# Splitting twelve weight units of the first mixing stage during the first down-projection

## The chip, the cores and the metric

The program runs on one core of one Trainium2 chip. The metric is the device time of one execution in microseconds (us). The engines named below are TensorE (PE in the profile, with PEld for its weight loads), VectorE (DVE), ScalarE (ACT), GpSimd (POOL) and the sync engine (SP), which issues most of the DMAs. Every engine works through its own list of instructions in the order in which the list was written; an instruction that waits holds up all that stand behind it on the same engine.

## The reference

One encoder layer runs over two independent sequences (`x_prompt` and `x_sample`) of 512 tokens and 1024 channels, with the same float32 weights for both:

```
x = x + 0.5 * swiglu(rms_norm(x, ffn1_norm), w_gate, w_up, w_down)      # D_FF = 2816
h = rms_norm(x, mix_norm)
proj = h @ w_in                        # 1024 x 4880: q, k, v, memory q, k, v, gates, output gate, two merge gates
att = grouped-query attention(proj);  mem = bidirectional mLSTM(proj)
x = x + (sigmoid(g_att) * (att @ w_up_att) + sigmoid(g_mlstm) * (mem @ w_up_mlstm)) @ w_out
x = x + 0.5 * swiglu(rms_norm(x, ffn2_norm), ...)
y = rms_norm(x, final_norm)
```

## The kernel before

Precision: each float32 operand is held as two reduced-precision parts, a high part (the value rounded) and a low part (the rest), and a product is made of three matmuls: high by high, high by low, low by high. Splitting a weight tile therefore costs one ACT instruction (the copy that rounds) and one DVE instruction (the subtraction).

Stages, in order: the up-projections of the first feed-forward block for both sequences; its down-projection `ffn_down`; the mixing stage of `x_prompt` (`mix(0, ...)`), then that of `x_sample` (`mix(1, ...)`); the second feed-forward block in the same two parts.

`ffn_down` works in 28 steps: seven products of a fast (Strassen-like) scheme for each of four chunks of the hidden width, taken in the order of `DOWN` (L539 to L544). A chunk holds three units of hidden rows, the third chunk two. In a step, `products` (L610) goes over four column blocks d, each in one PSUM bank, with three matmuls for each unit. When a block of a step is done, `flush_` (L655) adds the bank into a sum in SBUF: on ACT (L663) for some products of the first chunk, on DVE (L665) otherwise. Several products in a row build on the same bank, so PE may begin block d of the next step only when the flush of block d of this step has read the bank. `prep(i + 2)` (L601) makes the weight units of the step after next: `split` (L713) with ACT (L715) and DVE (L716) into a ring of eight unit buffers, and `load_right(i + 4)` issues the loads of the other operand, which were parked in DRAM, on SP. A unit buffer is free again when PE has ended the step that used it.

`e5` (L553) is a tile of the pool whose slots all have the size of the largest tile, 128 x 8 x 512; it is only half as large as its slot.

In the mixing stage the weights come in units of 128 columns of `w_in`. `load_w` (L281) serves both sequences. For `x_prompt` it loads the raw unit (512 KB, L271 on SP), splits it with ACT (L278) and DVE (L279) into a tile with the tag `w8`, of which there are four, and parks high and low part in DRAM with two DMAs on SP (L303). For `x_sample` the unit is found in the table `parked`, and two DMAs on SP (L293) bring both parts back. The lookup is:

```
if key in parked:
    d, shape = parked[key]
    w2 = wpool.tile(shape, F32R, tag="w8", bufs=4, name=nm("w"))
    for i in range(2):
        nc.sync.dma_start(f(w2[:, i]), d[:, i])
    return w2[:, 0], w2[:, 1]
```

In the attention part of `mix(0, ...)` the units of gates and of memory queries and keys are fed between the steps of the attention, by `among` (L1171) through `proj` (L814), whose matmuls have the lines L825 and L839.

Which order the instructions have on each engine is not the order of the code: a scheduler lays them out, and takes at each moment the instruction with the lowest place in the program (moved by `shifted`) among those that are ready by its own estimate. `pin` keeps some in the order of the program. `mix_consts` (L741) loads tables for the mixing stage on POOL's queue; it is called after step 7 of `ffn_down`.

Of the kernel before, what the change touches and what calls it, by code (L numbers as in the profile page):

```python
# [8 lines left out]
F32 = mybir.dt.float32  # L9
F32R = mybir.dt.float32r  # L10
I32 = mybir.dt.int32
AF = mybir.ActivationFunctionType
ALU = mybir.AluOpType
# [3 lines left out]
P = 128  # L17
S = 512
D = 1024
KD = D // P  # L20
# [6 lines left out]
def encoder(ctx, tc, I, outs):  # L27
    nc = tc.nc
    cpool = ctx.enter_context(tc.tile_pool(name="cpool", bufs=1))
    dpool = ctx.enter_context(tc.tile_pool(name="dpool", bufs=1, space=bass.MemoryType.DRAM))  # L30
# [11 lines left out]
    def nm(s):  # L42
        n_id[0] += 1
        return f"{s}_{n_id[0]}"
# [89 lines left out]
    def A(shape, dtype=F32, name="a"):  # L134
        return apool.tile(shape, dtype, tag="a", name=nm(name))
# [148 lines left out]
    parked = {}  # L284
# [23 lines left out]
    V_ = nc.vector  # L308
# [236 lines left out]
    DH = KD // 2  # L545
    n_steps = len(DOWN) * len(CHUNKS)

    def ffn_down(wd, rb, ring, tail, xres, done, at_step, hook, turned=None):
        n = n_steps
        rt = [A([P, 4, 2, S], F32R, "rt") for _ in range(3)]  # L550
        e16 = xs[2] = A([P, KD, S], F32, "e16")
        xs[0], xs[1] = A([P, KD, S], F32, "xs"), A([P, KD, S], F32, "xs")
        e5 = A([P, DH, S], F32, "e5")  # L553
        right = [[t[:, q] for q in range(3)] for t in rt] + [[t[:, 3] for t in rt]]
        w8 = [wpool.tile([P, 2, 2, S], F32R, tag="w8", bufs=4, name=nm("w")) for _ in range(4)]
        units = [t[:, i] for t in w8 for i in range(2)]
# [2 lines left out]
        free = [(0, t[:, 0:S], t[:, S:D]) for t in wr] + [(1, va, ha), (1, *v2)]  # L559
        s1s = ring.rows["s"]  # L560
        at = [0, 0]

        def load_right(i):
            if i < n:
                for q, fp in enumerate(CHUNKS[i // 7]):
                    nc.sync.dma_start(f(right[(i + 3) % 4][q]), rb[fp][DOWN[i % 7]])
# [13 lines left out]
        def refill():  # L580
            while order and free:
                key = order.pop(0)
                free.sort(key=lambda t: t[0])
                raws_[key] = load_raw(*key)
# [14 lines left out]
        def prep(i):  # L599

            if i >= n:  # L601
                return
            m, c = DOWN[i % 7], CHUNKS[i // 7]
            out = left[i] = []
            if m == T2_ and i > 2:
                sums(c)
            for fp in c:
                src = s1[fp] if m == T1 else raws_[fp, int(m in (B21, T4, B22))][1 + int(m in (T3, T4))]
                u = units[at[0] % 8]
                at[0] += 1  # L610
                split(src, u[:, 0, :], u[:, 1, :])
                out.append(u)
            if m in (T3, B22):
                for fp in c:
                    free.append(raws_.pop((fp, 0 if m == T3 else 1)))
                refill()
# [3 lines left out]
        def products(i, ts, ds=range(DH)):  # L620
            m = DOWN[i % 7]
            first = m in (B11, T2_, T1)
            grp = "Y" if m in (T2_, T3, T4) else "X"
            for d in ds:
                if first:
                    banks[grp, d] = (((PS, PS, PT, PT) if grp == "Y" else (MM, MM, MM, PO))[d])()
                p = banks[grp, d][:, ts]
                us = left[i]
                for q, u in enumerate(us):
                    r = right[(i + 3) % 4][q]  # L630
                    for k, (a, b) in enumerate(((0, 0), (0, 1), (1, 0))):
                        nc.tensor.matmul(p, u[:, a, d * P:(d + 1) * P], r[:, b, ts],  # L632
                                         start=(first and q == 0 and k == 0), stop=(q == len(us) - 1 and k == 2),
                                         skip_group_check=True)
                flush_(i, d, p, ts)

        def products_turned(i):

            us = left[i]
            for b in range(4):  # L640
                cuts = (0, S) if b < 3 else (0, S // 2, S)
                for j, c in enumerate(zip(cuts, cuts[1:])):
                    cs = slice(*c)
                    p = (MM, MM, MM, PO)[b - j]()
                    for q, u in enumerate(us):
                        r = right[(i + 3) % 4][q]
                        for k, (a, h) in enumerate(((0, 0), (0, 1), (1, 0))):
                            nc.tensor.matmul(p[:, cs], r[:, h, b * P:(b + 1) * P], u[:, a, cs],
                                             start=(q == 0 and k == 0),
                                             stop=(q == len(us) - 1 and k == 2), skip_group_check=True)  # L650
                    turned(b, j, len(cuts) - 2 - j, p[:, cs], cs)
# [44 lines left out]
        for i in range(n):  # L696
            if i == n - 1 and turned:
                products_turned(i)
            else:
                products(i, whole)  # L700
            prep(i + 2)
            load_right(i + 4)
            if i == 1:
                free.extend((1, *h4[k:k + 2]) for k in (0, 2))
                refill()
            if i == at_step:
                hook()

    def normed(xt, g, R, d):

        V_.scalar_tensor_tensor(xt, xt, g[:, d:d + 1], R, op0=ALU.mult, op1=ALU.mult)
# [8 lines left out]
    HM, DM = 4, 128  # L720
# [44 lines left out]
    win_v = w_in.rearrange("(k p) c -> p k c", p=P)  # L765
# [674 lines left out]
    def busy(n, idle):  # L1440

        for _ in range(n):
            pin(nc.tensor.matmul(idle, hot[:, 0:P], hot, start=True, stop=True))

    xbuf = [dpool.tile([P, KD, S], F32, name=f"xbuf{s}") for s in range(2)]
    x2buf = [dpool.tile([P, KD, S], F32, name=f"x2buf{s}") for s in range(2)]
    rbuf = [[[dpool.tile([P, 2, S], F32, name=f"rbuf{n}_{j}_{m}") for m in range(7)] for j in range(NF // 2)]
            for n in range(2)]
# [7 lines left out]
    up = Up(xc, I["ffn1_w_gate"][0], I["ffn1_w_up"][0], rbuf[0], 12)  # L1456
# [263 lines left out]
    tail = up.rest(raw0, 13, mix_gains)  # L1720
# [24 lines left out]
    def prep1(d):  # L1745
# [4 lines left out]
        normed(xt, gm, R[1], d)  # L1750
        split(xt, nhl[1][0][:, d, :], nhl[1][1][:, d, :])

    ffn_down(I["ffn1_w_down"][0], rbuf[0], up.ring, tail, xbuf, done1, 7, mix_consts)


    box()
# [56 lines left out]
    up = Up(xc, I["ffn2_w_gate"][0], I["ffn2_w_up"][0], rbuf[1], 10)  # L1813
# [21 lines left out]
    tail = up.rest(raw0)  # L1835
# [68 lines left out]
    def done2(s, d, th):  # L1904
# [5 lines left out]
        elif d == KD - 1:  # L1910
            turn1()

    ffn_down(I["ffn2_w_down"][0], rbuf[1], up.ring, tail, x2buf, done2, n_steps - 7, load_fn, turned=finish1)


# [40 lines left out]
```

## Time and profile before

| what | value |
|---|---|
| time, median of 3 runs | 2035.04 us (2034.21 to 2035.5) |
| the profiled execution | 2037.6 us, span 2035.8 us |
| PE busy | 2020.2 us of the span (99%) |
| DVE busy | 1584.0 us (78%) |
| ACT busy | 921.5 us (45%) |
| POOL busy | 111.1 us (5%) |
| first matmul of `ffn_down` | 437.76 us after the start |
| granted TensorE clock, mean | 0.999 |

The busy time of PE is made of modelled ends: matmuls overlap, so a duration of 389 ns does not mean that one starts every 389 ns. How fast PE goes is read from the starts. A row of a timeline names the start and the length in us, the engine, the line, the operation, what it writes and reads, and the number of equal instructions that it merges; in brackets stand the idle time before it and what ended it. A row of a stretch has, after the two ends and the length, the busy time of each engine with the number of its instructions, then the granted clock, the busy share of the 16 DMA engines, and GB/s.

### The profile page before, as it was taken

How to read it: one execution, taken by the hardware profiler on the slowest of the kernel's cores; microseconds unless marked ns; L12 is line 12 of the kernel's file. 1: busy time of each engine (PE TensorE's matmuls, PEld its weight loads, DVE VectorE, ACT ScalarE, POOL GpSimd, SP SyncE). 2: the span in 40 equal slices, each digit the busy share in tenths (PEclk: the TensorE clock that was granted, in tenths of full speed). 3: DMA queues.
4: the chain of work that ended last, by engine and by line, in shares of the span. 5: the costliest groups of instructions: out<-in, count | busy, mean ns of one | idle time of the engine just before them, and what ended most of it. 6: DMA issues, size and time to landing. Idle time of an engine off the chain costs nothing.

```text
span 2035.8 us, 26777 instructions
## 1 busy us (share of the span) xinstructions
PE 2020.2 (99%) x9185; PEld 1665.7 (82%) x9185; DVE 1584.0 (78%) x2828; ACT 921.5 (45%) x1675; POOL 111.1 (5%) x148
## 2 busy tenths in 40 slices
PE   9999999999999999999999999999999999999998
PEld 7888888888888888888888877888888888888887
DVE  7988888886797798776566867467798988786797
ACT  7644444442234577653325654245444444442224
POOL 0000000001003000100120000011000000000001
PEclk9999999999999999999999999999999999999999
DMA  9656565799766954868656668877565655689753
GB/s 312 197 171 216 177 218 182 237 334 364 271 214 225 294 169 148 259 208 302 211 166 209 214 189 268 274 228 228 173 206 166 217 177 179 205 332 352 269 196 119
DMA packets 334696, 462.17 MB, mean 227 GB/s; under 512 B 21384, under 2 KB 207840, under 8 KB 333280
## 3 DMA queue, kind: packets, MB, share of 16 engines
q1 hardware_dynamic: 329920, 446.08, 65.8%
q0 software_dynamic: 4480, 14.11, 2.0%
q8 instruction: 72, 1.18, 0.2%
q14 instruction: 64, 0.52, 0.1%
q10 hardware_dynamic: 160, 0.27, 0.0%
HBM read 292.44 MB, written 167.94 MB: 226 GB/s over the span
## 4 chain that ended last, share of the span: by engine, by line
PE 91%; DVE 3%; DMA 3%; ACT 2%; issue 1%; SPq 0%; DVEq 0%; ACTq 0%
PE mm L839 13%; PE pso L374 12%; PE pst L374 12%; PE mm L374 10%; PE mm L632 9%; PE pss L374 6%; PE pst L632 4%; PE pss L632 4%; PE mm L825 4%; PE mm L804 3%; PE pso L632 3%; PE pso L1148 1%; PE pss L1101 1%; PE pst L839 1%; PE pss L839 1%; PE pso L1360 1%
## 5 line engine op out<-in xcount | busy, mean ns | idle before, releaser
L374 PE MATMUL pst<-xc,w 128*128 128x512 f32 x1056 | 253.8, 389 | 1.2 <-ACT t L409 1.2
L374 PEld LDWEIGHTS pst<-xc,w 128*128 128x128 f32 x1056 | 198.1, 188 | 42.7 <-ACT t L409 1.6
L374 PE MATMUL mm<-xc,w 128*128 128x512 f32 x972 | 229.6, 390 | 1.6 <-ACT f L382 1.6
L374 PEld LDWEIGHTS mm<-xc,w 128*128 128x128 f32 x972 | 182.0, 188 | 39.6 <-ACT f L382 2.1
L632 PE MATMUL mm<-rt,w 128*128 128x512 f32 x765 | 178.7, 389 | 0.0
L839 PE MATMUL mm<-xh,w 128*128 128x512 f32 x560 | 176.1, 391 | 1.4 <-DMA w<-wpark 1.4
L332 ACT ACTIVATE w<-t 128x512 fp32r<-128x512 f32 x176 | 106.5, 627 | 135.7 <-issue 63.1
L632 PEld LDWEIGHTS mm<-rt,w 128*128 128x128 f32 x765 | 143.5, 188 | 29.8
L333 DVE TENSOR_TENSOR w<-t,w 128x512 fp32r<-128x512 f32 x176 | 117.8, 688 | 40.9 <-ACT w L332 39.1
L374 PE MATMUL pso<-xc,f 128*128 128x512 f32 x528 | 127.0, 389 | 0.0
L374 PE MATMUL pss<-xc,w 128*128 128x512 f32 x528 | 126.8, 389 | 0.0
L374 PE MATMUL pso<-xc,w 128*128 128x512 f32 x528 | 126.8, 389 | 0.0
L839 PEld LDWEIGHTS mm<-xh,w 128*128 128x128 f32 x560 | 104.8, 188 | 23.7 <-DMA w<-wpark 1.8
L374 PEld LDWEIGHTS pso<-xc,f 128*128 128x128 f32 x528 | 99.0, 188 | 21.0 <-DVE t L413 0.4
L374 PEld LDWEIGHTS pso<-xc,w 128*128 128x128 f32 x528 | 99.1, 188 | 20.6
L374 PEld LDWEIGHTS pss<-xc,w 128*128 128x128 f32 x528 | 99.1, 188 | 20.6
L825 PE MATMUL mm<-xh,w 128*128 128x512 f32 x336 | 111.9, 398 | 0.0
L839 PE MATMUL mm<-xl,w 128*128 128x512 f32 x280 | 109.6, 391 | 0.0
L715 ACT ACTIVATE w<-wr 128x512 fp32r<-128x512 f32 x72 | 45.1, 632 | 138.4 <-PE pso L632 64.8
L278 ACT ACTIVATE w<-wr 128x1024 fp32r<-128x1024 f32 (+1 forms) x64 | 65.3, 1030 | 80.4 <-issue 24.5
L279 DVE TENSOR_TENSOR w<-wr,w 128x1024 fp32r<-128x1024 f32 (+1 forms) x64 | 79.8, 1247 | 26.6 <-ACT w L278 15.7
L715 ACT ACTIVATE w<-t 128x512 fp32r<-128x512 f32 x82 | 51.8, 632 | 107.4 <-PE pst L632 62.4
(457 smaller groups left out, 4080.4 us busy)
## 6 DMA issues: line engine op xcount, KB each, us to landing
rt<-rbuf SPq DMA_DIRECT2D x154, 512.0 KB, 5.4
wpark<-w SPq DMA_DIRECT2D x88, 512.0 KB, 3.6
w<-wpark SPq DMA_DIRECT2D x88, 512.0 KB, 5.3
wr<-in_ffn_w_gate_dram SPq DMA_DIRECT2D x62, 512.0 KB, 5.4
rbuf<-tab SPq DMA_DIRECT2D x102, 256.0 KB, 4.0
wr<-in_ffn_w_up_dram SPq DMA_DIRECT2D x44, 512.0 KB, 4.6
rbuf<-f SPq DMA_DIRECT2D x72, 256.0 KB, 4.2
wr<-in_w_in_dram SPq DMA_DIRECT2D x36, 512.0 KB, 5.7
```

The source lines that it names most:

```text
L278: pin(nc.scalar.activation(hi, raw, AF.Copy))
L279: pin(lo_eng.tensor_tensor(lo, raw, f(hi), op=ALU.subtract))
L332: pin(nc.scalar.activation(t[:, 0], src, AF.Copy))
L333: pin(V_.tensor_tensor(t[:, 1], src, f(t[:, 0]), op=ALU.subtract))
L374: nc.tensor.matmul(p, a[:, k, :], xt[:, b, k, :], start=(first and k == 0 and i == 0), stop=(k == HK_ - 1 and i == 2), skip_group_check=True)
L632: nc.tensor.matmul(p, u[:, a, d * P:(d + 1) * P], r[:, b, ts], start=(first and q == 0 and k == 0), stop=(q == len(us) - 1 and k == 2), sk ...
L715: nc.scalar.activation(hi, src, AF.Copy)
L804: mark(nc.tensor.matmul(p[b][:, :N], a[:, k, bs], w_[:, kl, :], start=(k == 0 and i == 0), stop=(k == KD - 1 and i == 2)), (kl, b, i) == ( ...
L825: pin(nc.tensor.matmul(p[0], a[:, k, :], b, start=(k == 0 and i == 0), stop=(k == n - 1 and i == 2)))
L839: mark(nc.tensor.matmul(p, a[:, k, :], b, start=(k == 0 and i == 0), stop=last), last)
L1101: pin(nc.tensor.matmul(p, qT[:, h, b * P:(b + 1) * P], kv[:, hk * 2 + j, :], start=(j == 0), stop=(j == 1)))
L1148: pin(nc.tensor.matmul(pos[h], Vst[:, kb, h // 4, :], w, start=(kb == KBS[0] and i == 0), stop=(kb == KBS[3] and i == 1)))
```

## The change

`ffn_down` gets a list `aside` of twelve units of `w_in`. `e5` is allocated with twice the size, in the same slot, and its upper half is used as two buffers of 512 KB, `lo` and `hi`. After each step from step 10 on, one unit is written into the program: its raw values are loaded into `lo` on POOL's queue, ACT copies them to `hi`, DVE subtracts in place, and two DMAs on POOL's queue park both parts in DRAM under the key that the mixing stage looks up. There is one pair of buffers, so the load of the next unit overwrites what the two DMAs of this one read. In `mix(0, ...)` these twelve units are then found in `parked`: the raw load, the split and the two parking DMAs are gone there, and two loads stand in their place. `mix(1, ...)` is unchanged. Only the call in the first block passes a list.

```
-    def ffn_down(wd, rb, ring, tail, xres, done, at_step, hook, turned=None):
+    def ffn_down(wd, rb, ring, tail, xres, done, at_step, hook, turned=None, aside=()):
...
-        e5 = A([P, DH, S], F32, "e5")
+        e5_ = A([P, KD, S], F32, "e5")
+        e5, spare = e5_[:, 0:DH], e5_[:, DH:KD].rearrange("p (i a) c -> p i (a c)", i=2)
...
+        aside = list(aside)
+
+        def split_aside(view, key):
+            lo, hi = [spare[:, i].rearrange("p (k c) -> p k c", c=view.shape[2]) for i in range(2)]
+            nc.gpsimd.dma_start(lo, view)
+            nc.scalar.activation(hi.bitcast(F32R), lo, AF.Copy)
+            V_.tensor_tensor(lo.bitcast(F32R), lo, hi, op=ALU.subtract)
+            shape = [P, 2] + list(view.shape[1:])
+            parked[key] = d, _ = dpool.tile(shape, F32, name=nm("wpark")), shape
+            for i, t in enumerate((hi, lo)):
+                nc.gpsimd.dma_start(d[:, i], t)
...
             if i == at_step:
                 hook()
+            if i >= ASIDE and aside:
+                split_aside(*aside.pop(0))
+
+    ASIDE = 10
...
-    ffn_down(I["ffn1_w_down"][0], rbuf[0], up.ring, tail, xbuf, done1, 7, mix_consts)
+    ffn_down(I["ffn1_w_down"][0], rbuf[0], up.ring, tail, xbuf, done1, 7, mix_consts,
+             aside=[(win_v[:, :, c:c + P], ("in", c)) for c in
+                    (896, 1408, *(2832 + d * P for d in range(2)), *(2320 + h * P for h in range(HM)),
+                     *(2832 + d * P for d in range(2, 6)))])
```

In the changed kernel the lines behind the change have other numbers: the flushes are L676 (ACT) and L678 (DVE), the unit splits L732 (ACT) and L733 (DVE), the parts of the new function L568 (load), L569 (ACT), L570 (DVE) and L574 (parking).

Where the scheduler put this is seen at three places. POOL's list around the tables of the mixing stage, before (`hn` is the last of the small loads of the stage ahead, L744 to L754 are `mix_consts`):

```order
L738 TENSOR_SCALAR hn<-hn 128x4
L744 DMA tab_4218<-in_c_tri_dram 128x512
L745 DMA tab_4218<-in_c_mask_dram 128x256
L747 DMA f_302_4221<-in_c_rope_dram 128x8x64
L750 DMA gb_4223<-in_q_norm_dram 128x64
L752 TENSOR_SCALAR gb_4223<-gb_4223 128x64
```

and now (`e` is the tile of the two buffers):

```order
L755 TENSOR_SCALAR hn<-hn 128x4
L568 DMA e_276_3694<-in_w_in_dram 128x8x128
L574 DMA wpark_4393<-e_276_3694 128x1024 x2
L568 DMA e_276_3694<-in_w_in_dram 128x8x128
L574 DMA wpark_4453<-e_276_3694 128x1024 x2
L568 DMA e_276_3694<-in_w_in_dram 128x8x128
L761 DMA tab_4218<-in_c_tri_dram 128x512
L762 DMA tab_4218<-in_c_mask_dram 128x256
L764 DMA f_302_4221<-in_c_rope_dram 128x8x64
L767 DMA gb_4223<-in_q_norm_dram 128x64
L574 DMA wpark_4509<-e_276_3694 128x1024 x2
```

Two units and the load of a third stand ahead of the tables, though the program writes the tables three steps earlier; load and parking follow each other in turns, and the other nine units follow behind.

ACT's list at the end of step 0 of `ffn_down` (the flush of its last block, from the bank `pso`), before:

```order
L663 ACTIVATE e_273_3691<-pso_3811 128x512
L715 ACTIVATE w_3695<-wr_3701 128x512
L715 ACTIVATE w_3696<-wr_3701 128x512
L715 ACTIVATE w_3697<-wr_3702 128x512
L715 ACTIVATE w_3697<-t_18_279 128x512
```

and now:

```order
L676 ACTIVATE e_273_3691<-pso_3811 128x512
L569 ACTIVATE e_276_3694<-e_276_3694 128x1024
L732 ACTIVATE w_3695<-wr_3701 128x512
L732 ACTIVATE w_3696<-wr_3701 128x512
L732 ACTIVATE w_3697<-wr_3702 128x512
L732 ACTIVATE w_3697<-t_18_279 128x512
```

The first of the twelve copies stands behind the flushes of step 0, not behind step 10, and the unit splits of step 3 and 4 behind it; the other eleven follow at distances of three to six unit splits at first, and four at the end.

DVE's list around the twelfth of the subtractions (`mm` and `pso` of 45xx are the banks of step 15, `pss_4660` and `pss_4668` those of the first two blocks of step 16):

```order
L678 SCALAR_TENSOR_TENSOR xs_3692<-mm_4572,xs_3692 128x512
L678 SCALAR_TENSOR_TENSOR xs_3692<-mm_4580,xs_3692 128x512
L570 TENSOR_TENSOR e_276_3694<-e_276_3694 128x1024
L678 SCALAR_TENSOR_TENSOR xs_3692<-pso_4588,xs_3692 128x512
L733 TENSOR_TENSOR w_3697<-t_6_267,w_3697 128x512
L678 SCALAR_TENSOR_TENSOR e_273_3691<-pss_4660,e_273_3691 128x512
L733 TENSOR_TENSOR w_3697<-t_7_268,w_3697 128x512
L678 SCALAR_TENSOR_TENSOR e_273_3691<-pss_4668,e_273_3691 128x512
```

The subtraction is new there; the flushes of step 15 and 16 and the unit splits stand around it in the order that they had before.

## The prediction

> **What bounds the kernel now.** I read the totals of the page first, then the busy time by stretch, then the starts of the matmuls.
>
> ```profile
> span 2035.8 us, 26777 instructions
> PE 2020.2 (99%) x9185; PEld 1665.7 (82%) x9185; DVE 1584.0 (78%) x2828; ACT 921.5 (45%) x1675; POOL 111.1 (5%) x148
> ```
>
> PE is busy in 99% of the span: a wait that PE does not have today is paid in full, and work that leaves ACT, DVE or SP gains only what PE idles for it. The profiled execution is 2037.6 us, its span and 1.8 us outside it, and lies 2.6 us above the median of 2035.04; I add the sum to the span and carry it over to the median. About 0.2% (4 us) is what a measurement of this kernel can tell from no change.
>
> By stretch (after the ends and the length: busy time and number of instructions, granted clock, DMA share, GB/s): three of `ffn_down`, and the attention of `mix(0, ...)`.
>
> ```profile
> core 0: us, PE busy (x) PEld busy (x) DVE busy (x) ACT busy (x) POOL busy (x), PEclk, DMA share, GB/s
> 437.80:494.90 57.10, 57.10 (x254) 47.28 (x253) 41.92 (x65) 22.38 (x39) 8.67 (x12) 1.00 0.98 367
> 494.90:552.00 57.10, 57.10 (x253) 47.28 (x252) 38.60 (x60) 13.29 (x21) 0.00 (x0) 1.00 0.75 267
> 552.00:590.00 38.00, 38.00 (x169) 31.48 (x168) 32.61 (x53) 8.81 (x14) 0.00 (x0) 1.00 0.69 242
> 690.00:800.00 110.00, 109.75 (x543) 89.47 (x542) 100.19 (x202) 73.57 (x142) 0.00 (x0) 1.00 0.58 192
> ```
>
> The place that work is taken from, 690 to 800, has a PE that idles 0.25 us; the place that it goes to has a PE that never idles, and in its first 57 us DMA engines that are full already (0.98).
>
> Two starts of steps, by PE's timeline:
>
> ```profile
> 437.76 6.28 PE L632 MATMUL mm<-rt,w 128*128 128x512 f32 x27
> 445.92 6.28 PE L632 MATMUL mm<-rt,w 128*128 128x512 f32 x27
> 552.00 4.24 PE L632 MATMUL mm<-rt,w 128*128 128x512 f32 x18
> 557.44 4.24 PE L632 MATMUL mm<-rt,w 128*128 128x512 f32 x18
> 568.32 2.88 PE L632 MATMUL pss<-rt,w 128*128 128x512 f32 x12
> ```
>
> A step of three units takes 8.16 us, one of two units (steps 14 to 20) 5.44 us. Step 14 begins at 552.00, step 17 at 568.32.
>
> **What the change takes from the mixing stage.** Twelve copies, twelve subtractions, twelve raw loads and 24 parkings, by the row for the raw tile and the one for the parked parts between 690 and 800:
>
> ```profile
> L279 DVE TENSOR_TENSOR w<-wr,w x13: 1201/1218/1227, 690.0 to 791.7; 128x1024 fp32r<-128x1024 f32 x13
> L278 ACT ACTIVATE w<-wr x12: 1040/1058/1062, 689.7 to 790.6; 128x1024 fp32r<-128x1024 f32 x12
> L271 SPq DMA_DIRECT2D wr<-in_w_in_dram x12: 384/452/1826, 693.5 to 783.5; - x12
> DMA to landing us min/median/max: 4.4/4.7/8.1
> ```
>
> ```profile
> L303 SPq DMA_DIRECT2D wpark<-w x26: 319/320/704, 689.9 to 793.0; - x26
> DMA to landing us min/median/max: 2.6/3.2/4.7
> ```
>
> That is 12 x 1.06 = 12.7 us of ACT and 12 x 1.22 = 14.6 us of DVE, all under a PE that idles 0.25 us in 110 us. The matmuls of these units stand in the groups by shape with 1.4 us lost over the whole program:
>
> ```profile
> L839 PE MATMUL mm<-xh,w 128*128 128x512 f32 x560 | 176.1, 391 | 1.4 <-DMA w<-wpark 1.4
> ```
>
> Since ends are modelled, some idleness may hide in the busy time: PE misses 15.6 us (2035.8 - 2020.2) in the whole span, of which a share by length (110 / 2035.8) is 0.8 us. I put the gain at 1.5 us, between none and 3 us (twice the 1.4 of the row).
>
> **What it adds: a chain through one buffer pair.** By the order, ACT's first copy stands behind the flush of step 0, the twelfth subtraction on DVE between the flushes of step 15. ACT and DVE take their instructions in order, so each copy that is not ready holds up the flushes and unit splits behind it, and PE waits for those. The rows at both ends, of ACT and of DVE, and that of the unit splits around them:
>
> ```profile
> 447.35 0.61 ACT L663 ACTIVATE e<-pso 128x512 f32<-128x512 f32 x1
> ```
>
> ```profile
> 562.18 1.31 ACT L715 ACTIVATE w<-t 128x512 fp32r<-128x512 f32 x2 [4.08 <-PE pso L632]
> ```
>
> ```profile
> 563.45 0.69 DVE L665 SCALAR_TENSOR_TENSOR xs<-pso,xs 128x512 f32<-128x512 f32 x1
> ```
>
> The first copy can begin at 447.35 + 0.61 = 448.0; its load, issued when the buffer is free at about 437.8, has ten microseconds. The latest start of the twelfth without harm: behind its subtraction DVE has the flush of step 15's last block, a unit split and the flush of step 16's first block, which PE needs at 568.3. Three at 0.69 are 2.1, the subtraction 1.22, the copy 1.06, two handovers about 0.2: 568.3 - 4.6 = 563.7, and I take 563. So eleven cycles must fit into 563 - 448 = 115 us, 10.45 us for each. (The same reckoning gives 506 for the sixth, so the line is nearly straight.)
>
> A cycle is: raw load, copy, subtraction, handover to POOL, landing of the low part's parking, since the next load overwrites what that reads. The floor of it, with the fastest landings of the rows above and the one place where POOL sends what DVE has just made:
>
> ```profile
> 1047.74 0.69 DVE L1426 SCALAR_TENSOR_TENSOR f<-mm,f 128x512 f32<-128x512 f32 x1
> ```
>
> ```profile
> 1048.73 0.56 POOL L1427 DMA_DIRECT2D x2buf<-f  x1 [4.86 <-DVE f L1426]
> ```
>
> DVE ends at 1048.43, so the handover is 0.30. Floor: 4.4 + 1.06 + 1.22 + 0.30 + 2.6 = 9.6 us. That is only 0.85 us under the allowance, and it has no load from others and SP's issue times in it. POOL's own, from the tables of the mixing stage:
>
> ```profile
> 467.88 0.60 POOL L744 DMA_DIRECT2D tab<-in_c_tri_dram  x1 [134.76 <-DMA wr<-in_ffn_w_down_dram]
> 469.02 0.91 POOL L747 DMA_DIRECT2D f<-in_c_rope_dram  x1
> ```
>
> The second moves 128 x 8 pieces, like a raw unit: 0.91 against SP's 0.45 above, +0.5, so 10.1. Then the load of the DMA engines. The operand `rt` (512 KB, as here) landed thus from 500 to 600 and from 445 to 500:
>
> ```profile
> L566 SPq DMA_DIRECT2D rt<-rbuf x38: 319/320/627, 501.9 to 598.4; - x38
> DMA to landing us min/median/max: 3.2/4.4/6.0
> ```
>
> ```profile
> L566 SPq DMA_DIRECT2D rt<-rbuf x21: 319/320/447, 445.3 to 495.1; - x21
> DMA to landing us min/median/max: 5.8/8.6/13.8
> ```
>
> After 500 the median is 1.2 above the minimum; on both legs that is 10.1 + 2.4 = **12.5 us** a cycle. The new traffic itself (1.5 MB in 12.5 us is 126 GB/s on top of 242 to 267) fills the engines to about the 367 of the first stretch, so this is rather too little than too much: from 10.9 (0.4 on each leg) to 15 (half the excess of the first stretch on each leg).
>
> In the first stretch I go by POOL's own transfers of 256 KB, those of `x2buf` in the quiet and the table `tri` at 467.88:
>
> ```profile
> L1427 POOL DMA_DIRECT2D x2buf<-f x16: 540/557/599, 1033.7 to 1391.4; - x16
> DMA to landing us min/median/max: 2.3/4.1/12.5
> ```
>
> ```profile
> tab<-in_c_tri_dram POOLq DMA_DIRECT2D x1, 256.0 KB, 5.9
> ```
>
> 5.9 against 2.3: +3.6 on each leg, 10.1 + 7.2 = 17.3; since a lone transfer in a queue may pass `rt`'s crowded one I take **16**, for the three cycles that begin before 495 (10.9 if the excess of `tri` is its own, 18 if both legs wait as `rt` does).
>
> Against the change speaks a rule of the Trainium skill, "DMA: Bandwidth & Descriptors", section "Issuing engines are not separate DMA queues": another issuing engine brings no DMA engines of its own, so transfers compete for the same sixteen. The row of `tri` agrees (5.9 us on POOL's queue while SP filled the engines).
>
> Between the third load and its parking POOL also has the mixing stage's tables and their scalings: +1 us.
>
> **The sum.** Twelfth copy: 448 + 3 x 16 + 1 + 8 x 12.5 = 597. Less the allowed 563: PE is held up 34 us in all, in pieces from the third unit on, and a stall once taken is not given back by the engines behind, since POOL's chain does not wait for PE. (Sixth: 448 + 49 + 25 = 522 against 506, 16 us: the last decides.) After a stall PE starts slowly, as the first matmuls of the program do:
>
> ```profile
> 1.63 2.93 PE L1443 MATMUL pst<-xc 128*128 128x512 f32 x6 [1.63 <-DVE xc L1528]
> ```
>
> Six took 2.93; at the pitch of a step (8.16 us for 36) and one modelled tail of 0.39 they would take 1.5. So a long stall costs up to 1.4 more; most here are short, +1 in all. 34 + 1 - 1.5 = +33.5: the profiled execution's span goes to 2069, the median to **2068 us**. With the low cycles: 448 + 11 x 10.9 + 1 = 569, +6; with the high ones: 448 + 54 + 1 + 120 = 623, +60.
>
> **Rivals.**
>
> *The chain fits.* The load of others costs POOL's transfers nothing because a queue with one transfer in it is served beside the crowded one; the cycle is then 9.6 to 10.4, under 10.45. For it: the floor itself; against it: `tri`, 3.6 above its like, and 0.5 of issue. Only the gain of at most 3 us is left: 2032 to 2035, say 2033.5. Not slower. Chance 0.13. It decides for a cycle below 10.45 on the mean. The rule of the Trainium skill that gives this result stands in "DMA: Bandwidth & Descriptors", section "Anatomy of one DMA — SWDGE (gpsimd) path": it fits a DMA from this engine as 2.0 us plus bytes over 436 GB/s: an estimate of 3.2 us for 512 KB and of about 9 us a cycle, with which nothing would stall. By that rule the time of `x2buf` in the quiet agrees (2.3 for 256 KB, by the fit 2.6), in the full stretch `tri` does not (5.9).
>
> *The operand comes late instead.* `rt` is asked for about three steps ahead (24.5 us) and landed within 13.8 us in the worst case, so some 10 us are spare. Three units of 1.5 MB in the full stretch are 4.7 MB, at 367 GB/s 12.8 us more to move. PE waits for `rt` some 3 to 9 us, the chain less than I reckon: 2038 to 2044. Against it: the stretch behind has a quarter of the engines free. Chance 0.09.
>
> *The loads in the mixing stage come late.* Where the units follow each other, two loads of 512 KB must land for each unit of 24 matmuls (24 / 36 x 8.16 = 5.4 us):
>
> ```profile
> w<-wpark SPq DMA_DIRECT2D x88, 512.0 KB, 5.3
> ```
>
> 5.3 a load against 4.7 for the raw one, one more load and no splitting behind it; at worst 3 us for each of three units in a row, +9: 2044. The row of L839, with 1.4 us lost to such loads in all, speaks against it. Chance 0.05.
>
> *The change doesn't do what it says* (the units are found too late to spare the splits, or copies stand elsewhere): the order lists show the raw loads gone and the loads in their place, so 2035, chance 0.03.
>
> **Chances and range.** My forecast has 0.70, the rivals 0.13, 0.09, 0.05 and 0.03. The likeliest case's own range is 2042 to 2092; it is the whole range too, since it leaves out the first and last rival (0.16) and holds part of the second and third. Slower by over 0.2%: 0.69 of the forecast, 0.07 of the late operand, 0.04 of the late loads, 0.80 together. Within 0.2%: most of the first rival (0.10), the last, and scraps, 0.16. Faster: 0.04.
>
> **What would show it.** In the changed profile PE's starts from step 2 to 17 would lie apart by more than 8.16 or 5.44 us, the waits of PE put down to ACT or DVE flushes and, behind them, those of ACT's copy to the load into `e`; the twelve loads on POOL would follow each other by 16 us at first and about 12.5 later. The first rival shows as distances near 10 and a step 17 at 568; the second as PE's waits put down to `rt`; the third as waits for `wpark` in the mixing stage. I am wrong in kind if the copies are ready before their place in ACT's list, wrong in size if the distances are not 16 and 12.5.

## The result and the profile after

The changed kernel takes 2092.47 us (median of 4 runs, 2090.0 to 2092.87) against 2034.85 us for the kernel before, measured beside it: a ratio of 1.0278, 95% interval 1.0266 to 1.0291, 57.6 us more. The direction was forecast; the loss was forecast at 33 us, and the median lies 0.5 us above the upper end of the range (2092), with single runs on both sides of that end.

The totals of its page, and the busy time by stretch (ends, length, busy time and instructions of each engine, granted clock, DMA share, GB/s). The first stretch is as long as that of before, the other two follow it:

```profile
span 2091.1 us, 26773 instructions
PE 2035.9 (97%) x9185; PEld 1676.1 (80%) x9185; DVE 1579.2 (76%) x2828; ACT 919.4 (44%) x1675; POOL 133.1 (6%) x184
```

```profile
437.10:494.20 57.10, 42.90 (x177) 34.68 (x176) 27.41 (x44) 18.16 (x31) 9.38 (x15) 0.91 1.01 371
494.20:610.00 115.80, 90.35 (x347) 71.96 (x345) 59.55 (x92) 24.52 (x39) 18.73 (x29) 0.87 0.78 279
610.00:647.00 37.00, 34.12 (x142) 27.75 (x143) 31.69 (x51) 10.07 (x16) 3.06 (x5) 0.95 0.83 292
```

Where PE was busy for all 57.1 us, it is now busy for 42.9, with 177 matmuls instead of 254. Step 17 begins at 627.05, counted from the first matmul of the stage 59.4 us later than before, and from there on the distance grows by little more than 0.1 us. The whole loss is made between steps 3 and 17.

What PE waited for between 437 and 700 (engine and line, releaser: total, times, longest):

```profile
PE pst L645 <- DVE xs L678: 9.5, 1, 9.5
PE pss L645 <- ACT w L732: 6.5, 1, 6.5
PE mm L645 <- DVE xs L678: 6.4, 1, 6.4
PE mm L645 <- issue: 6.3, 1, 6.3
PE pst L645 <- ACT e L676: 4.7, 1, 4.7
PE pso L645 <- DVE e L678: 3.7, 1, 3.7
PE pso L645 <- DVE xs L678: 2.7, 1, 2.7
PE mm L645 <- ACT e L676: 2.4, 1, 2.4
PE pss L645 <- issue: 0.4, 1, 0.4
```

They are flushes (L676, L678) and unit splits (L732): work of ACT and DVE that has itself nothing to do with the twelve units. The two rows put down to "issue", for which the profile names no releaser, are flushes too. Step 13 begins at 588.38, 0.10 us after DVE has ended the flush that frees the bank of its first block, and step 17 begins 0.10 us after such a flush as well:

```profile
587.59 0.69 DVE L678 SCALAR_TENSOR_TENSOR e<-mm,e 128x512 f32<-128x512 f32 x1
```

What holds all this up is one level further back, in the waits of all engines:

```profile
ACT e L569 <- DMA e<-in_w_in_dram: 117.3, 11, 16.5
DVE e L570 <- ACT e L569: 89.5, 11, 15.1
POOL e L568 <- DMA wpark<-e: 43.8, 10, 8.0
```

ACT stands 117 us before eleven of the twelve copies, waiting for their load; POOL waits to issue the load until the parking has landed. One cycle of it, in the chain of work that ended last (start, length, what):

```profile
498.29 9.42 DMA e<-in_w_in_dram
507.82 1.06 ACT e L569
508.90 1.24 DVE e L570
510.43 4.67 DMA wpark<-e
515.38 7.90 DMA e<-in_w_in_dram
```

Transfer, copy, subtraction, transfer, transfer: no gap of more than 0.3 us between them. The first, fourth, fifth, sixth and last copy on ACT's timeline (start, length; in brackets the idle time before it) give the length of the cycles:

```profile
447.16 1.07 ACT L569 ACTIVATE e<-e 128x1024 fp32r<-128x1024 f32 x1
...
507.82 1.06 ACT L569 ACTIVATE e<-e 128x1024 fp32r<-128x1024 f32 x1 [8.30 <-DMA e<-in_w_in_dram]
...
523.38 1.06 ACT L569 ACTIVATE e<-e 128x1024 fp32r<-128x1024 f32 x1 [11.49 <-DMA e<-in_w_in_dram]
533.81 1.06 ACT L569 ACTIVATE e<-e 128x1024 fp32r<-128x1024 f32 x1 [7.81 <-DMA e<-in_w_in_dram]
...
622.83 1.06 ACT L569 ACTIVATE e<-e 128x1024 fp32r<-128x1024 f32 x1 [7.95 <-DMA e<-in_w_in_dram]
```

From first to last 175.7 us, 15.97 a cycle, where 10.45 were allowed. The three first take 60.7 us (20.2 each), the other eight 115.0 (14.4 each). The shortest of all, from 523.38 to 533.81, takes 10.43.

### The profile page after: what moved, and what is told of

It reads as the page before. It is cut to its first block, busy times and chain, and to the rows that moved or that the text cites. A ratio compares the mean times of both kernels' runs of the same rounds, so it can differ in the third digit from the quotient of the medians.

```text
span 2091.1 us, 26773 instructions
## 1 busy us (share of the span) xinstructions
PE 2035.9 (97%) x9185; PEld 1676.1 (80%) x9185; DVE 1579.2 (76%) x2828; ACT 919.4 (44%) x1675; POOL 133.1 (6%) x184
## 4 chain that ended last, share of the span: by engine, by line
PE 86%; DMA 8%; DVE 2%; issue 2%; ACT 2%; SPq 0%; POOL 0%; ACTq 0%; POOLq 0%; DVEq 0%
PE mm L856 15%; PE pst L374 11%; PE pso L374 11%; PE mm L374 10%; PE mm L645 6%; PE pss L374 5%; PE mm L842 5%; PE mm L821 3%; PE pss L645 3%; PE pst L645 3%; DMA e<-in_w_in_dram 2%; PE pso L645 2%; DMA wpark<-e 2%; PE pss L1118 1%; PE pso L1165 1%
## 5 line engine op out<-in xcount | busy, mean ns | idle before, releaser
L645 PE MATMUL mm<-rt,w 128*128 128x512 f32 x765 | 186.4, 400 | 15.0 <-DVE xs L678 6.4
L645 PEld LDWEIGHTS mm<-rt,w 128*128 128x128 f32 x765 | 148.7, 195 | 48.0 <-DVE xs L678 6.8
L332 ACT ACTIVATE w<-t 128x512 fp32r<-128x512 f32 x176 | 106.6, 627 | 135.4 <-issue 63.1
L645 PE MATMUL pst<-rt,w 128*128 128x512 f32 x396 | 97.4, 399 | 14.2 <-DVE xs L678 9.5
L645 PE MATMUL pss<-rt,w 128*128 128x512 f32 x396 | 95.2, 394 | 6.9 <-ACT w L732 6.5
L645 PEld LDWEIGHTS pst<-rt,w 128*128 128x128 f32 x396 | 76.4, 194 | 31.1 <-DVE xs L678 9.9
L645 PEld LDWEIGHTS pss<-rt,w 128*128 128x128 f32 x396 | 75.2, 190 | 23.4 <-ACT w L732 7.7
```

Of the source, the lines that this page charges most:

```text
L332: pin(nc.scalar.activation(t[:, 0], src, AF.Copy))
```

## The experiments

A measure that all of them share is PE's lag: the start of a step's first matmul, counted from the first matmul of the stage, less the same in the kernel before. In us:

| kernel | step 4 | step 8 | step 14 | step 18 | last matmul |
|---|---|---|---|---|---|
| the change | 6.4 | 30.6 | 53.3 | 59.5 | 59.5 |
| `tight` | 3.3 | 24.8 | 44.4 | 55.9 | 55.9 |
| `spaced_twelve` | 0.0 | 4.5 | 13.2 | 20.7 | 27.3 |
| `dma_only` | 0.0 | 0.3 | 6.5 | 6.5 | 27.9 |
| `tight_no_reload` | 0.0 | 5.5 | 11.6 | 11.6 | 11.6 |
| `dma_eight` | 0.0 | 0.1 | 6.1 | 6.1 | 6.1 |
| `late_five` | 0.0 | 0.0 | 0.0 | 4.7 | 4.7 |
| `late_four` | 0.0 | 0.0 | 0.0 | 0.0 | 0.0 |
| `one_unit` | 0.0 | 0.0 | 0.0 | 0.0 | 0.0 |

The first theory was the one of the prediction: the chain is longer than the distance of the copies, and the in-order lists of ACT and DVE pass that on to PE. The rival: the 18.9 MB of added transfers starve PE of its own operand.

**`one_unit`: the mixing stage alone.**

```
             if i >= ASIDE and aside:
+                key = aside[0][1]
                 split_aside(*aside.pop(0))
+                parked.update((k, parked[key]) for _, k in aside)
+                aside.clear()
```

> Only the first of the twelve units is split and parked in the down-projection; the other eleven keys point to its parked parts, so eleven units have the wrong values and the mixing stage runs exactly as in the change. Theory: one cycle holds nothing up, so this is the gain of the mixing stage alone, 0 to 3.5 us: 2031.5 to 2035 us. Rival (the mixing stage waits for the two loads of 512 KB that replace one): 2036 to 2044 us, with waits for the parked parts before the matmuls of the projections.

2034.11 us against 2035.87 for the kernel before, ratio 0.9988 (0.9979 to 0.9997): 1.8 us faster, with an interval from 0.6 to 4.3. So all that the change could win is about two microseconds, 4.3 at most by this interval. Part of it is seen in the mixing stage: counted from the last matmul of the down-projection, PE's 601st matmul, some 118 us later, comes 1.0 us earlier in this run than in the kernel before, and 1.1 in the change. The loads do not come late: the projections' matmuls lose less to them than the 1.4 us of before (group by shape, idle time last).

```profile
L859 PE MATMUL mm<-xh,w 128*128 128x512 f32 x560 | 176.2, 391 | 1.0 <-DMA w<-wpark 1.0
```

**`dma_only`: the transfers without the splits.**

```
             nc.gpsimd.dma_start(lo, view)
-            nc.scalar.activation(hi.bitcast(F32R), lo, AF.Copy)
-            V_.tensor_tensor(lo.bitcast(F32R), lo, hi, op=ALU.subtract)
...
-            for i, t in enumerate((hi, lo)):
+            for i, t in enumerate((lo, lo)):
```

> The copy and the subtraction of the twelve units are left out, and the raw values are parked twice; all transfers of the change stay, in the same queue and the same buffer. Theory (ACT and DVE held up in their order make the loss, not the transfers): 2031 to 2037 us, and PE's waits in the down-projection below 3 us, though the loads on GpSimd's queue still take 6 to 9 us each to land. Rival (transfers starve PE): 2060 us or more with PE's waits put down to its own operand; something between, about 2040 to 2045, if both have a part.

2060.58 us, ratio 1.0117 (1.0101 to 1.0132). Neither theory had this: nearly half of the loss is there with no copy in ACT's list. The lag has two parts, and the waits of PE name them:

```profile
PE pst L643 <- DVE e L676: 19.0, 1, 19.0
PE mm L643 <- issue: 3.0, 1, 3.0
PE mm L643 <- DMA rt<-rbuf: 1.1, 1, 1.1
```

By step 14, 6.5 us are lost, where PE waits for its operand once and, in the row put down to "issue", for a flush (the next run shows why that was late). Then nothing more is lost until step 24, and then come 21 us at one place. There ACT stands before the split of the mixing stage's input:

```profile
640.07 2.56 ACT L143 ACTIVATE xh<-xs,gain 128x512 fp32r<-128x512 f32 x4 [26.81 <-DMA wpark<-e]
```

`xh` waits for the last parking, which left POOL at 636.20 and landed 3.8 us later; it can do so only as the next user of the slot of `e5`, whose upper half the buffers are. The unit splits behind it on ACT then hold up DVE and PE. Even with no splits a cycle takes about 17 us here, twelve of them 203 us (437.3 to 640.0), and the slot is wanted at about 613. I had not seen this waiter at all. The next run takes it away.

**`dma_eight`: the same, ending after eight units.**

```
                 split_aside(*aside.pop(0))
+                if len(aside) == 4:
+                    parked.update((k, d) for (_, k), d in zip(aside, [*parked.values()][-4:]))
+                    aside.clear()
```

> As the run with transfers alone (no copies and subtractions, raw values parked twice), but after the eighth unit the chain ends, and the last four keys point to parked parts of earlier units. Its chain of about 17 us a cycle ends near 575 us instead of 640. Theory (the late stall of 21 us came from the slot of the two buffers, which the input of the mixing stage waits for until the last parking has landed): that stall is gone, and about 6.5 us of PE waiting for its operands stay, less the gain of the mixing stage: 2037 to 2042 us. Rival (the transfers late in the stage cost by themselves): a stall stays after 600 us, 2048 us or more.

2040.25 us, ratio 1.0024 (1.0014 to 1.0034), within the expectation. The late stall is gone, the early part stays, 6.1 us:

```profile
505.02 5.05 PE L643 MATMUL mm<-rt,w 128*128 128x512 f32 x21 [1.39 <-DMA rt<-rbuf]
547.16 8.00 PE L643 MATMUL mm<-rt,w 128*128 128x512 f32 x27 [2.42 <-issue]
```

The first row is a wait for the operand; with it PE is 1.8 us late, and stays so up to step 12. The second is something else. Step 13 begins 0.10 us after DVE's flush of the first block of step 12, and that flush stands on DVE behind an addition that waits for raw weights of the down-projection itself:

```profile
542.76 0.69 DVE L605 TENSOR_TENSOR t<-wr,t 128x512 f32<-128x512 f32 x1 [7.49 <-DMA t<-in_ffn_w_down_dram]
```

```profile
546.38 0.68 DVE L676 SCALAR_TENSOR_TENSOR e<-mm,e 128x512 f32<-128x512 f32 x1
```

So the transfers by themselves, with no copy in the lists, cost PE about 6 us in two ways: 1.8 by its operand, and 4.3 at the flush behind a raw weight that came late to DVE. The expectation had put all of it down to the operand; that the time fits is in part luck. In the stretch 500 to 560 of this run the DMA engines are full and PE is not:

```profile
500.00:560.00 60.00, 56.19 (x241) 45.74 (x240) 38.33 (x62) 13.29 (x21) 11.38 (x19) 0.97 1.01 376
```

**`tight` and `tight_no_reload`: one leg of the chain less at the same places.** `tight` keeps the copies and subtractions at written places near those of the change; `tight_no_reload` takes from it all loads but the first.

```
-            nc.scalar.activation(hi.bitcast(F32R), lo, AF.Copy)
-            V_.tensor_tensor(lo.bitcast(F32R), lo, hi, op=ALU.subtract)
+            pin = tc.keep_in_program_order
+            pin(nc.scalar.activation(hi.bitcast(F32R), lo, AF.Copy))
+            pin(V_.tensor_tensor(lo.bitcast(F32R), lo, hi, op=ALU.subtract))
...
-            if i >= ASIDE and aside:
+            if i in ASIDE and aside:
...
-    ASIDE = 10
+    ASIDE = (0, 2, 3, 5, 6, 7, 8, 10, 11, 12, 13, 15)
```

and in `tight_no_reload` beside it

```
-            nc.gpsimd.dma_start(lo, view)
+            if len(aside) == 11:
+                nc.gpsimd.dma_start(lo, view)
```

> All twelve units in full as in the change, with the copies kept behind steps 0, 2, 3, 5, 6, 7, 8, 10, 11, 12, 13 and 15, which is near the places that the scheduler gave them in the change. It is the control of the next run: both theories expect about the change, 2080 to 2100 us.

> As the run before it, with the same places, but only the first unit is loaded: the other eleven copies, subtractions and parkings work on what is in the buffers, so their values are wrong. ACT, DVE and two thirds of the transfers are as in the change, one leg of the chain is gone. Theory (the length of the chain against the distance of the places): a cycle of subtraction, handover and landing, 1.2 + 0.3 + 4.5 to 8.5 us plus 1 for the copy, 7 to 11 us, fits places 8 to 16 us apart with 10 us of slack: 2034 to 2043 us. Rival (copies and subtractions on ACT and DVE, or the transfers, cost by themselves): two thirds of the loss or all of it, 2070 us or more.

`tight`: 2090.76 us, ratio 1.0273 (1.0255 to 1.0292), as the change. `tight_no_reload`: 2045.97 us, ratio 1.0055 (1.0041 to 1.0069). With the same copies, subtractions and parkings at the same places, and a third of the added bytes gone, 45 of 55 us are gone. The DMA engines are full all the same (share 1.02 from 437 to 500, 0.97 from 500 to 560), and the copies follow each other by 10.4 us on the mean. The time is 3 us above the upper end of the expectation. Of the waits of PE that remain, the first is a flush behind the tenth subtraction, which itself waited 4.29 us for a parking; the second is the operand:

```profile
PE mm L647 <- DVE e L680: 4.1, 1, 4.1
PE mm L647 <- DMA rt<-rbuf: 3.1, 3, 1.4
```

So neither the work on ACT and DVE nor two thirds of the bytes carry the loss, and `dma_only`, with all of the bytes, had lost 6.5 us before its late stall; the length of the cycle against the distance of the places does.

**`spaced_twelve`, `late_five`, `late_four`: the places further apart.** As `tight`, with only the list changed:

```
+    ASIDE = (1, 3, 5, 7, 9, 11, 13, 16, 19, 22, 24, 26)    spaced_twelve
+    ASIDE = (8, 11, 14, 17, 20)                            late_five
+    ASIDE = (8, 11, 15, 20)                                late_four
```

> All twelve units are split as in the change, but the copy and the subtraction of each are kept at fixed places in the lists of ACT and DVE: behind steps 1, 3, 5, 7, 9, 11, 13, 16, 19, 22, 24 and 26, that is one per 16.3 us instead of one per about 10.4. Theory (the copies stand ahead of their data, and hold up flushes behind them): cycles of 19 to 22 us at first run behind their places by 3 to 6 us, which the roughly 10 us between a place and the matmul that needs it take up, later cycles of 11 to 17 fit: 2031 to 2038 us, PE idle in the down-projection below 5 us. Rival (the extra 18 MB of transfers in the down-projection starve PE of its own operands): the same bytes move in the same stage, so half or more of the loss stays, 2060 us or more.

2062.59 us, ratio 1.0129 (1.0115 to 1.0142): half of the loss is gone, though the bytes are the same, but far from all. The expectation was too low because a cycle at full DMA engines is longer than I had put it: the first three took 18.6, 22.4 and 23.2 us against places 16.3 apart, and after them the fourth came later than its slack. The largest waits of PE:

```profile
PE pso L646 <- DVE e L679: 6.5, 1, 6.5
PE mm L646 <- DVE xs L679: 4.2, 2, 3.6
PE mm L646 <- issue: 3.1, 1, 3.1
```

> Only five of the twelve units are split in the down-projection, the other seven stay in the mixing stage as before; the copies stand behind steps 8, 11, 14, 17 and 20, 16 to 24 us apart, and the last parking lands before the tiles of the mixing stage ask for the slot. Theory (a chain that fits costs nothing, and what is left is the gain of the mixing stage): 2033 to 2036.5 us, no wait of PE over 1 us in the down-projection. Rival (the traffic itself costs): 5/12 of the 6.5 us that the run with transfers alone lost before its late stall, +3 us: 2038 to 2039.

2039.59 us, ratio 1.0016 (1.0007 to 1.0025): missed. Only 0.2 us are lost up to step 17, then 4.5 us at once. The fourth copy is due 16.3 us behind the third, in steps of two units, and waits 6 us for its load:

```profile
569.55 1.06 ACT L570 ACTIVATE e<-e 128x1024 fp32r<-128x1024 f32 x1 [6.00 <-DMA e<-in_w_in_dram]
```

```profile
572.52 2.41 PE L646 MATMUL pss<-rt,w 128*128 128x512 f32 x6 [2.62 <-DVE e L679]
```

The third copy had itself come 18.3 us after the second, after waiting 1.86 us for its load. Of the 4.5 us, 2.6 are PE's wait; the rest is lost by matmuls at a lower clock behind it (granted 0.97 from 560 to 620). The rival had the time nearly right (2038 to 2039), but not the mechanism: no wait of PE is put down to its operand.

> Four of the twelve units are split in the down-projection, behind steps 8, 11, 15 and 20, 24 to 27 us apart; the other eight stay in the mixing stage. The run with five lost 4.7 us at its fourth unit, whose place was 16.3 us behind the third, while the cycle took 16.5 to 18.3. Theory (a place further apart than the cycle costs nothing): PE's lag in the down-projection is under 0.5 us, and the time is 2033.5 to 2036.5 us, since a third of the mixing stage's gain is 0.6 us. Rival (the transfers cost by themselves, in proportion): 2037 us or more, with PE's waits put down to its own operand.

2033.88 us against 2035.52, ratio 0.9996 (0.9987 to 1.0005): no difference that can be measured, as expected. A round from one copy to the landing of the next load takes 17.5 to 18.5 us here, less than the distance of the places. PE has no wait in the stage, though 6.3 MB are moved there beside its own:

```profile
500.00:560.00 60.00, 60.00 (x267) 49.67 (x266) 44.62 (x69) 17.01 (x26) 5.10 (x8) 1.00 0.93 320
560.00:620.00 60.00, 60.00 (x266) 49.71 (x265) 57.40 (x89) 19.14 (x31) 6.54 (x6) 1.00 0.77 268
```

It does not beat the kernel before, and by `one_unit` no version of this kind can by more than about 2 us (4.3 at the end of the interval).

**`mix_on_pool`: the queue by itself.** The kernel before, with the parked units' raw loads issued by GpSimd:

```
-            nc.sync.dma_start(raw[:, :, c:c + v.shape[2]], v)
+            (nc.gpsimd if pool else nc.sync).dma_start(raw[:, :, c:c + v.shape[2]], v)
...
-        raw = fetch_w(view)
+        raw = fetch_w(view, pool=park)
```

> The kernel before, with the raw loads of the weights of the first mixing stage issued by GpSimd instead of the sync engine: the same transfers on the other queue, to price the queue itself. If GpSimd's queue is slow by itself, a 512 KB load in 512 B pieces lands there in 6 us or more between 690 and 800 us, against 4.4 to 8.1 us with median 4.7 on the sync engine's queue; if the load of the DMA engines made the loads of the change slow (median 7.6 us), it lands in 5 to 5.5 us, the issue of 0.9 us instead of 0.45 included. The time stays within 10 us of before.

2035.39 us (one run). From 690 to 800 us the loads of 512 KB, issued by POOL (in the fence: duration of the issue, then landing of all loads of the raw tile, one of another shape among them):

```profile
L271 POOL DMA_DIRECT2D wr<-in_w_in_dram x12: 704/882/891, 692.6 to 784.7; - x12
...
DMA to landing us min/median/max: 4.8/5.5/9.6
```

5.5 against the sync engine's 4.7, and 0.43 of that is the longer issue. The queue is not what made the loads of the change slow. There, the load on POOL and PE's operand on the sync engine's queue between 500 and 620 landed thus (changed kernel, lines of the loads and of `rt`):

```profile
L568 POOL DMA_DIRECT2D e<-in_w_in_dram x12: 908/909/952, 437.8 to 616.3; - x12
...
DMA to landing us min/median/max: 4.4/7.6/9.4
```

```profile
L579 SPq DMA_DIRECT2D rt<-rbuf x29: 319/326/1256, 503.7 to 614.7; - x29
DMA to landing us min/median/max: 3.2/6.4/9.7
```

The operand's median was 4.4 before: the two streams slow each other.

## Why the prediction was right in kind and too small

**The mechanism** was as forecast: the copies stand ahead of their data, PE waits for flushes and unit splits that are queued behind them, and the twelfth decides. That the length of the chain is the cause is shown by `tight_no_reload` (same work at the same places, shorter cycle) and by `spaced_twelve` (all the work and all the bytes, places further apart: 27 us lost instead of 58). `late_four`, with places further apart than its rounds, loses nothing, but moves only a third of the bytes.

**The mis-sized term is the cycle.** The sum put three at 16 and eight at 12.5 us, with 1 us for the tables between; measured are 60.7 us for the three (against 49) and 115.0 for the eight (against 100). The tables cost the chain nothing: the fourth load left POOL 0.29 us after the parking had landed. With the first copy at 447.2 instead of 448, the twelfth stood at 622.8 instead of 597. The rest of the sum holds: the latest harmless start, 563 by the times of before and 562.3 by this execution's earlier first matmul (437.07 instead of 437.76), gives 622.8 - 562.3 = 60.5 us of lag; measured are 59.5. The 1.0 us between them lies in the path from the twelfth copy to PE, for which the sum allowed 5.3 us (568.3 - 563) and which took 4.2 (622.83 to 627.05).

The high cycles of the sum, 18 and 15 us, put the twelfth copy at 623, which is right only because two deviations cancel (20.2 and 14.4 measured). And the range was drawn too narrow: with the +1 and the -1.5 of the sum, the low and the high cycles give 2040.5 and 2094.5, not 2042 and 2092, and the result lies in the part left off; no reason for that is given. The 15 is itself low: half the excess of `rt` in the first stretch (8.6 against 3.2) on each leg gives 15.5.

What made the first three cycles long: the loads landed in 8.4 us on the mean and the low parts' parkings in 7.7. The rows of the sum give 8.5 (4.4 + 0.5 + 3.6) and 6.2 (2.6 + 3.6), 17.3 for the cycle, and I then took 16, since a lone transfer might pass the crowded queue; that was too low. The first subtraction also came 3.2 us late, behind other work of DVE.

What made the other cycles long: from the fifth load on, the loads landed in 6.8 us on the mean (forecast: 5.6, and 0.5 of issue), the low parts' parkings before them in 4.5 (forecast: 3.8), and the handovers that I had left out (landing to POOL's issue 0.3, landing to ACT 0.1) add 0.4. The prediction had expected the new traffic to fill the engines. On the mean it did not: the share was 0.78 at 279 GB/s from 494 to 610, against 0.75 at 267 in the second stretch of before: PE, held up, asks for less (29 loads of `rt` between 500 and 620 instead of 44). The trace shows what lies beside the slow loads: five of these eight were issued within 3 us behind loads of `rt` on the sync engine and landed in 6.5 to 8.4 us; the three that were not landed in 4.4, 4.8 and 6.2. No run varies this, so that it is the reason is not shown.

The floor, 10.1 with POOL's issue, was too low as well. The shortest cycle, with a load of 4.40 us and a parking of 3.07, both near the fastest of the run (4.4 and 2.9), took 10.43 us against the 10.45 allowed: the chain had no room even where its transfers were fast.

The Trainium skill's "DMA: Bandwidth & Descriptors", section "Anatomy of one DMA — SWDGE (gpsimd) path", gives an estimate of 3.2 us for 512 KB by its fit. The fastest parkings of the change come to it (2.9); its loads take 4.4 at the fastest and 7.6 in the median, those of `mix_on_pool` 5.5. As a price under load it is less than half of what the loads of the change took. The section "Issuing engines are not separate DMA queues" of the same page of the Trainium skill, by which transfers run on the same engines whoever issues them, agrees with the change (`rt` 4.4 to 6.4).

**The restart at a slow clock** I had added as +1. It is far larger, and costs nothing here. PE's waits sum to 42.6 us of the 59.5; the other 16.9 are matmuls at a lower clock (granted 0.91 and 0.87 in the first two stretches), as the nine behind the longest wait, which take 4.21 us where nine without a wait take 2.20 (granted 0.50 from 491.9 to 496.1):

```profile
480.21 2.20 PE L645 MATMUL pst<-rt,w 128*128 128x512 f32 x9
491.91 4.21 PE L645 MATMUL pst<-rt,w 128*128 128x512 f32 x9 [9.50 <-DVE xs L678]
```

Since the chain sets the end, slow matmuls only fill time in which PE would have waited anyway; the lag is that of the chain (60.5 reckoned, 59.5 measured) with nothing on top. Where PE waits for no later copy, as in `late_five`, the slow matmuls are paid: 4.5 us lost at a wait of 2.6.

**The gain in the mixing stage**, put at 1.5 us, is 1.8 (0.6 to 4.3) by `one_unit`.

**The rivals.** The chain that fits fell with the 15.97 us a cycle. The late operand is real, but small: `dma_eight` loses 6.1 us (forecast 3 to 9), but only 1.8 of them by the operand; the other 4.3 come by the late raw weight on DVE, which the rival did not have, so that the 6.1 fit is luck. In the change itself no wait of PE is put down to `rt`, and the 6.7 us of "issue" are flushes. The late loads in the mixing stage fell with `one_unit`. The change does what it says: the raw loads of 512 KB from `w_in` on the sync engine go from 36 to 24, and twelve stand on POOL. What I had not listed is the waiter behind the last parking, the slot of `e5`; in `dma_only` it cost 21 us. In the change it cost nothing, since PE and with it the mixing stage's input (667.78) came later than the chain's end (630.76).

**Open.** Why some loads land late was not varied, as said above. How much the late operand and the late raw weights would cost beside a chain that fits with all twelve units was not tried either. The 6.7 us that `spaced_twelve` loses after step 25 are read from its trace alone: the eleventh subtraction waits 4.1 us for its copy, and the flush for which step 27 waits (the row put down to "issue", 3.1) stands on DVE behind seven instructions of the mixing stage's input (655.88 to 661.63). No engine but POOL waits for a parking there, so the slot of `e5` has no visible part in it.

## What to carry to other kernels

Work that is moved into a stage "with idle engines" must be costed as a chain: add up load, work, handovers and the landing that frees the buffer, and compare one round with the distance at which the in-order lists reach its instructions; where the round is longer, the difference is paid once per round by whatever is queued behind, however idle those engines are on the mean. Do not take a leg's duration from the mean share of the DMA engines: here the mean hardly rose (0.75 to 0.78) while the loads took half as long again as their fastest (6.8 against 4.4). And ask first what the whole move can win: here one run with the receiving side alone says two microseconds.

## What the runs showed that was not expected

- A slot that is shared with a parking buffer has a second price: the next user of the slot waits for the last transfer out of it (26.8 us on ACT in `dma_only`, 21 us of PE's lag).
- PE can lose 17 us to a lower granted clock within waits without the time being longer for it, as long as another chain sets the end.
- Added traffic can hold up PE without touching its operands: a raw weight that lands late stops DVE for 7.5 us in `dma_eight`, and the flush behind it stops PE.
- A wait of PE that the profile puts down to "issue" could be named in five of these runs: PE starts 0.10 us after DVE's flush of the same bank.
- With full DMA engines (share 1.02, 382 GB/s, 437.4 to 566.2 in `dma_eight`), a round of one 512 KB load and the parking of two parts took 18.4 us on the mean of seven with nothing else in it, 1.8 times the shortest full round with its copy and subtraction in it (10.43 us).
